# Lp pooling on one Trainium2 core: whole-load squares and sums against chunks, with group 0 stored in two parts

## The chip, the core and the metric

The kernel runs on one NeuronCore of a Trainium2 chip. The core has several engines that run side by side, each with its own instruction queue: ScalarE (ACT in the profile), VectorE (DVE), GpSimd (POOL), TensorE (PE, not used here) and SyncE (SP), which here only starts DMA transfers. Data moves between the chip's main memory (HBM) and the core's working memory (SBUF, 128 partitions) on 16 DMA engines, which all queues share. The metric is the time of one execution on the device in microseconds (us); lower is better.

## The reference: what is computed

The input `x` has the shape 32 x 256 x 4096 in float32, `p` is 2 and the window is 4. Every four neighbours along the last axis give one output:

```python
for i in range(out_length):                      # out_length = 4096 // 4
    window = np.abs(x[:, :, 4*i:4*i + 4]) ** p   # p = 2: squares
    result[:, :, i] = (np.mean(window, axis=-1)) ** (1.0 / p)
```

With p = 2 this is the square root of the mean of four squares. 134.22 MB are read and 33.55 MB written. Nothing is used twice, and windows never overlap, so the input may be taken as one flat row of numbers, cut anywhere at a multiple of four.

## The kernel before, in words

**Tiling.** The flat input is spread over 128 partitions, 262144 columns for each. It is taken in 22 loads: 18 of 13184 columns (6592 KB each), then three of 6592 and one of 5056. A load goes into a slot. There are three slots of 13184 columns (`x_tiles`, L62), used in rotation; slot 18 holds two of the small loads and slot 19 the last two. Loads form groups (`groups`, L41): nine groups of two full loads, one of the three loads of 6592, and one of the last load. The outputs of a group lie together in one of two output tiles (`o_tiles`, L63), and are written to HBM by one store for the group. The outputs of groups 9 and 10 lie in slot 2 (`in_x`, L43), which no later load needs.

**Steps of a load.** ACT squares its columns in place (L123). DVE adds each four neighbours into the output tile: in the first 17 loads with one reduce (L93), from load 17 on with two additions of pairs (L99 and L101). ACT then takes the root with a scale of 1/4, in place in the output tile (L86). The list of chunks in `slots` (L39, L40) says how many columns one square and one sum take: all 13184 in loads 0 to 15, two halves in loads 16 and 17, the whole load in loads 18 to 20, two halves of 2528 in load 21.

**Order.** The order of instructions on each engine is that of the program (`manual_schedule`, L64), and the engines wait for each other by semaphores. In the main loop a root is not emitted at once. It is put on the list `pending`, once per group in general, and comes off it after the square and the sum of the next chunk have been emitted (`LAG`, L44 and L125). The names `FINE` and `ENDS` make the last groups root in smaller pieces: after load 19 (with it the outputs of loads 18 and 19), after load 20, and after each half of load 21.

**Transfers.** Loads are started from SP (L77), and a load of a slot waits until DVE has summed what was in it. Stores of groups 0 to 6 are started from ACT, right after the group's root (L88). The stores of groups 7 to 10 (`late`, L42) are started from SP behind all loads (L137). SP works in order: a store that waits for its root holds up what stands behind it in that queue. The first reduce into an output tile waits until the store of the group that had it before has landed.

Of the kernel before, what the change touches and what calls it, by code (L numbers as in the profile page):

```python
# [1 line left out]

# [4 lines left out]


@with_exitstack
def kernel(  # L10
    ctx: ExitStack,
    tc: tile.TileContext,
    x: bass.AP,
    p: float,
    kernel_size: int,
    out: bass.AP,
):

    nc = tc.nc

    assert float(p) == 2.0, "kernel specialized for p == 2"
    k = int(kernel_size)
    assert k == 4, "kernel specialized for kernel_size == 4"

    P = nc.NUM_PARTITIONS  # L30
    fp32 = mybir.dt.float32
    Act = mybir.ActivationFunctionType
    xf = x.rearrange("b c l -> (b c l)")
    of = out.rearrange("b c l -> (b c l)")
    total = xf.shape[0] // P

    W, O_W = 13184, 6592
    X_SLOTS, O_SLOTS = 3, 2
    slots = [[(W, [W])]] * 16 + [[(W, [6592, 6592])]] * 2  # L39
    slots += [[(6592, [6592]), (6592, [6592])], [(6592, [6592]), (5056, [2528, 2528])]]  # L40
    groups = [2] * 9 + [3, 1]  # L41
    late = {7, 8, 9, 10}  # L42
    in_x = {9: (2, 0), 10: (2, 4944)}  # L43
    FINE, ENDS, LAG = {21}, {19, 20}, 1  # L44
    PAIRS = 17


    loads = [(s, sum(w for w, _ in slot[:j]), *slot[j]) for s, slot in enumerate(slots)
             for j in range(len(slot))]
    n = len(loads)  # L50
    assert sum(w for _, _, w, _ in loads) == total

    firsts = [sum(groups[:g]) for g in range(len(groups))]
    assert sum(groups) == n
    group_of = [g for g, count in enumerate(groups) for _ in range(count)]
    columns = [sum(w for _, _, w, _ in loads[firsts[g]:firsts[g] + groups[g]])
               for g in range(len(groups))]

    x_pool = ctx.enter_context(tc.tile_pool(name="x_pool", bufs=1))
    o_pool = ctx.enter_context(tc.tile_pool(name="o_pool", bufs=1))  # L60

    x_tiles = [x_pool.tile([P, W], fp32, name=f"xt{j}") for j in range(X_SLOTS)]  # L62
    o_tiles = [o_pool.tile([P, O_W], fp32, name=f"ot{j}") for j in range(O_SLOTS)]  # L63
    ctx.enter_context(tc.manual_schedule())  # L64

    def block(flat, g, div):
        at, width = sum(columns[:g]) * P // div, columns[g] * P // div
        return flat[at:at + width].rearrange("(p w) -> p w", p=P)

    xs = {}  # L70

    def load(i):
        s, at, w, _ = loads[i]
        v = x_tiles[s % X_SLOTS][:, at:at + w]
        g = group_of[i]
        src = sum(loads[j][2] for j in range(firsts[g], i))
        nc.sync.dma_start(out=v, in_=block(xf, g, 1)[:, src:src + w])  # L77
        xs[i] = v

    ots = {}  # L80

    def store(g, queue):
        queue.dma_start(out=block(of, g, k), in_=ots[g])  # L83

    def root(g, o, ends):
        nc.scalar.activation(out=o, in_=o, func=Act.Sqrt, scale=1.0 / k)  # L86
        if ends and g not in late:
            store(g, nc.scalar)  # L88

    def total_sum(o, v, i):  # L90
        add = mybir.AluOpType.add
        if i < PAIRS:
            nc.vector.tensor_reduce(  # L93
                out=o, in_=v.rearrange("p (n j) -> p n j", j=k),
                axis=mybir.AxisListType.X, op=add,
            )
            return
        h = v.rearrange("p (m t) -> p m t", t=2)
        nc.vector.tensor_tensor(out=h[:, :, 0], in0=h[:, :, 0], in1=h[:, :, 1], op=add)  # L99
        q = v.rearrange("p (n j) -> p n j", j=k)  # L100
        nc.vector.tensor_tensor(out=o, in0=q[:, :, 0], in1=q[:, :, 2], op=add)  # L101

    ahead = 0
    while ahead < n and loads[ahead][0] < X_SLOTS - 1:
        load(ahead)
        ahead += 1
    pending = []
    done = 0
    for i in range(n):
        s, _, w, chunks = loads[i]  # L110
        while ahead < n and loads[ahead][0] < s + X_SLOTS:
            load(ahead)
            ahead += 1
        g = group_of[i]
        if i == firsts[g]:
            t, first = (o_tiles[g % O_SLOTS], 0) if g not in in_x else (x_tiles[in_x[g][0]], in_x[g][1])
            ots[g] = t[:, first:first + columns[g] // k]
            summed = rooted = 0
        assert sum(chunks) == w
        c = 0  # L120
        for step in chunks:
            v = xs[i][:, c:c + step]
            nc.scalar.activation(out=v, in_=v, func=Act.Square)  # L123
            total_sum(ots[g][:, summed:summed + step // k], v, i)
            while pending and pending[0][0] <= done - LAG:  # L125
                root(*pending.pop(0)[1:])
            done += 1
            c += step
            summed += step // k
            ends = summed == columns[g] // k  # L130
            if ends or i in FINE or (i in ENDS and c == w):
                pending.append((done - 1, g, ots[g][:, rooted:summed], ends))
                rooted = summed
    for job in pending:
        root(*job[1:])
    for g in sorted(late):
        store(g, nc.sync)  # L137


# [1 line left out]
_INS = ['x', 'p', 'kernel_size']  # L141
_OUTS = [((32, 256, 1024), 'float32')]

_NUMBERS = {'p': 2.0, 'kernel_size': 4}


# [26 lines left out]
```

## Time and profile before

The median of 3 runs is 397.92 us (397.87 to 398.24).

| | |
|---|---|
| profiled execution, its own time | 398.24 us |
| its span, from the first instruction to the last | 396.2 us |
| ACT busy | 281.7 us in 40 instructions |
| DVE busy | 275.0 us in 32 instructions |
| DMA, mean rate over the span | 423 GB/s |
| one square of 13184 columns (L123) | 11.19 us |
| one reduce of 13184 columns (L93) | 13.89 us |
| one root of 6592 columns (L86) | 5.68 us |
| a full load, from issue to landing (median) | 31.7 us |
| a store from ACT, from issue to landing (median) | 27.0 us |

"Busy" is the time in which an engine executed an instruction; starting a DMA and waiting are not counted. The span is shorter than the execution's time by what lies ahead of the first instruction and behind the last one. The columns of the windows view are: the stretch and its length, busy time of DVE, ACT and POOL in it with the number of instructions, the clock granted to TensorE, the mean share of time in which the 16 DMA engines were at work, and the rate in GB/s. A packet is counted with its whole size where it starts, so single microseconds may show shares over 1. In the table of waits a row gives the engine and line that waited, what ended the wait, the time in total, how often, and the longest. SPq and ACTq are the queues from which DMAs are started. In lines of the timeline, the first number is the start, the second the duration; square brackets give the idle time before it and what ended that.

### The profile page before, as it was taken

What the parts mean: (1) busy time and instruction counts of PE and PEld (TensorE: products, weight loads), DVE (VectorE), ACT (ScalarE), POOL (GpSimd) and SP (SyncE); (2) the same over time, 40 slices, a digit from 0 to 9 for tenths busy, and PEclk for the clock granted to TensorE, in tenths of its full rate; (3) what the DMA queues carried; (4) which work ended last, traced back from release to release, by engine and by line L of the source; (5) the groups of instructions that cost most, each with busy time, mean ns of one, the idle gap of its engine ahead of it and who ended that gap; (6) DMA issues with size and microseconds to landing.
All of it is one profiled execution on the core that took longest, in us unless ns stands there. A gap on an engine that the chain in (4) does not pass through costs nothing.

```text
span 396.2 us, 192 instructions
## 1 busy us (share of the span) xinstructions
DVE 275.0 (69%) x32; ACT 281.7 (71%) x40; POOL 0.2 (0%) x4
## 2 busy tenths in 40 slices
DVE  0008898685959286929691969396919697699594
ACT  1095689929880998199709972996299639997973
POOL 0000000000000000000000000000000000000000
DMA  8999999999999999999999999999999999999967
GB/s 341 431 442 453 442 437 426 381 431 466 423 407 442 437 426 453 426 437 418 466 426 426 426 415 445 434 453 399 458 453 410 453 426 426 410 445 416 447 269 321
DMA packets 4752, 167.77 MB, mean 423 GB/s; under 512 B 528, under 2 KB 528, under 8 KB 656
## 3 DMA queue, kind: packets, MB, share of 16 engines
q1 hardware_dynamic: 3744, 144.15, 84.5%
q10 hardware_dynamic: 1008, 23.63, 13.8%
HBM read 134.22 MB, written 33.55 MB: 423 GB/s over the span
## 4 chain that ended last, share of the span: by engine, by line
DMA 47%; ACT 24%; DVE 22%; issue 6%; SPq 0%; ACTq 0%
DMA xt<-in_x_dram 47%; ACT xt L123 18%; DVE ot L93 14%; ACT ot L86 6%; DVE xt L99 4%; DVE xt L101 2%; DVE ot L101 2%; ACT xt L86 1%; ACT L86 0%; SPq L77 0%; ACTq L83 0%
## 5 line engine op out<-in xcount | busy, mean ns | idle before, releaser
L93 DVE TENSOR_REDUCE ot<-xt 128x3296 f32<-128x13184 f32 (+1 forms) x18 | 236.2, 13123 | 110.6 <-ACT xt L123 108.9
L123 ACT ACTIVATE xt<-xt 128x13184 f32<-128x13184 f32 (+2 forms) x25 | 223.1, 8937 | 102.0 <-DMA xt<-in_x_dram 100.2
L86 ACT ACTIVATE ot<-ot 128x6592 f32<-128x6592 f32 x9 | 51.2, 5683 | 2.9 <-DVE ot L101 2.9
L99 DVE TENSOR_TENSOR xt<-xt 128x3296 f32<-128x3296 f32 (+1 forms) x7 | 20.9, 2986 | 5.7 <-ACT xt L123 5.7
L101 DVE TENSOR_TENSOR xt<-xt 128x1648 f32<-128x1648 f32 (+1 forms) x5 | 12.1, 2411 | 0.2
L86 ACT ACTIVATE xt<-xt 128x632 f32<-128x632 f32 (+2 forms) x4 | 6.0, 1492 | 5.0 <-DVE xt L101 5.0
L101 DVE TENSOR_TENSOR ot<-xt 128x1648 f32<-128x1648 f32 x2 | 6.2, 3119 | 0.1
L123 ACT ACT_TABLE_LOAD x1 | 1.3, 1283 | 0.7 <-PEq L154 0.7
L86 ACT ACT_TABLE_LOAD x1 | 1.3, 1283 | 0.0
L154 POOL MEMSET const-uint8-127<- 128x1 uint8 x1 | 0.1, 102 | 0.0
L154 POOL MEMSET const-bfloat16-1.0<- 128x1 bf16 x1 | 0.1, 101 | 0.0
L154 POOL MEMSET const-float32-0.0<- 128x1 f32 x1 | 0.1, 98 | 0.2 <-issue 0.2
L154 POOL MEMSET const-float32-1.0<- 128x1 f32 x1 | 0.1, 98 | 0.0
## 6 DMA issues: line engine op xcount, KB each, us to landing
xt<-in_x_dram SPq DMA_DIRECT2D x18, 6592.0 KB, 31.7
out_dram<-ot ACTq DMA_DIRECT2D x7, 3296.0 KB, 27.0
xt<-in_x_dram SPq DMA_DIRECT2D x3, 3296.0 KB, 27.8
out_dram<-ot SPq DMA_DIRECT2D x2, 3296.0 KB, 25.0
xt<-in_x_dram SPq DMA_DIRECT2D x1, 2528.0 KB, 23.0
out_dram<-xt SPq DMA_DIRECT2D x1, 2472.0 KB, 7.3
out_dram<-xt SPq DMA_DIRECT2D x1, 632.0 KB, 3.1
```

What stands on the lines that cost most here:

```text
L86: nc.scalar.activation(out=o, in_=o, func=Act.Sqrt, scale=1.0 / k)
L93: nc.vector.tensor_reduce(out=o, in_=v.rearrange("p (n j) -> p n j", j=k), axis=mybir.AxisListType.X, op=add,)
L99: nc.vector.tensor_tensor(out=h[:, :, 0], in0=h[:, :, 0], in1=h[:, :, 1], op=add)
L101: nc.vector.tensor_tensor(out=o, in0=q[:, :, 0], in1=q[:, :, 2], op=add)
L123: nc.scalar.activation(out=v, in_=v, func=Act.Square)
L154: nc = _bacc.Bacc("TRN2", target_bir_lowering=False, num_devices=1)
```

## The change

Every load is now cut into chunks: the 18 full ones into 4416, 4384 and 4384 columns, the loads of 6592 into two of 3296, and the last one, as before, into two of 2528. Every chunk has one square, one reduce and one root; the root of a chunk stands on ACT behind the square of the next chunk. The additions of pairs, `FINE`, `ENDS`, `LAG` and `PAIRS` are gone. The first chunk of group 0 is stored by itself as soon as it is rooted (1104 outputs, 4.4 KB per partition), and the rest of that group in a second store (5488 outputs); the other groups still have one store each. The tiles of slots and outputs are no longer made once: each load slot and each group asks a rotating pool for one, and the outputs of groups 9 and 10 take the next two places in the rotation of the slots. In the changed program the loads of slot 19 wait for the last reduce of slot 16; before, each waited for one of its two reduces.

```diff
--- before.py
+++ after.py
@@ -36,13 +37,11 @@
 
     W, O_W = 13184, 6592
     X_SLOTS, O_SLOTS = 3, 2
-    slots = [[(W, [W])]] * 16 + [[(W, [6592, 6592])]] * 2
-    slots += [[(6592, [6592]), (6592, [6592])], [(6592, [6592]), (5056, [2528, 2528])]]
+    slots = [[(W, [4416, 4384, 4384])]] * 18
+    slots += [[(6592, [3296, 3296])] * 2, [(6592, [3296, 3296]), (5056, [2528, 2528])]]
     groups = [2] * 9 + [3, 1]
     late = {7, 8, 9, 10}
-    in_x = {9: (2, 0), 10: (2, 4944)}
-    FINE, ENDS, LAG = {21}, {19, 20}, 1
-    PAIRS = 17
+    in_x = {9, 10}
 
 
     loads = [(s, sum(w for w, _ in slot[:j]), *slot[j]) for s, slot in enumerate(slots)
@@ -56,22 +55,22 @@
     columns = [sum(w for _, _, w, _ in loads[firsts[g]:firsts[g] + groups[g]])
                for g in range(len(groups))]
 
-    x_pool = ctx.enter_context(tc.tile_pool(name="x_pool", bufs=1))
-    o_pool = ctx.enter_context(tc.tile_pool(name="o_pool", bufs=1))
-
-    x_tiles = [x_pool.tile([P, W], fp32, name=f"xt{j}") for j in range(X_SLOTS)]
-    o_tiles = [o_pool.tile([P, O_W], fp32, name=f"ot{j}") for j in range(O_SLOTS)]
+    x_pool = ctx.enter_context(tc.tile_pool(name="x_pool", bufs=X_SLOTS))
+    o_pool = ctx.enter_context(tc.tile_pool(name="o_pool", bufs=O_SLOTS))
     ctx.enter_context(tc.manual_schedule())
 
     def block(flat, g, div):
         at, width = sum(columns[:g]) * P // div, columns[g] * P // div
         return flat[at:at + width].rearrange("(p w) -> p w", p=P)
 
+    slot_tiles = {}
     xs = {}
 
     def load(i):
         s, at, w, _ = loads[i]
-        v = x_tiles[s % X_SLOTS][:, at:at + w]
+        if at == 0:
+            slot_tiles[s] = x_pool.tile([P, W], fp32, name="xt")
+        v = slot_tiles[s][:, at:at + w]
         g = group_of[i]
         src = sum(loads[j][2] for j in range(firsts[g], i))
         nc.sync.dma_start(out=v, in_=block(xf, g, 1)[:, src:src + w])
@@ -79,33 +78,26 @@
 
     ots = {}
 
-    def store(g, queue):
-        queue.dma_start(out=block(of, g, k), in_=ots[g])
+    stored = {}
+
+    def store(g, queue, until=None):
+        first = stored.get(g, 0)
+        until = columns[g] // k if until is None else until
+        queue.dma_start(out=block(of, g, k)[:, first:until], in_=ots[g][:, first:until])
+        stored[g] = until
 
     def root(g, o, ends):
         nc.scalar.activation(out=o, in_=o, func=Act.Sqrt, scale=1.0 / k)
         if ends and g not in late:
             store(g, nc.scalar)
-
-    def total_sum(o, v, i):
-        add = mybir.AluOpType.add
-        if i < PAIRS:
-            nc.vector.tensor_reduce(
-                out=o, in_=v.rearrange("p (n j) -> p n j", j=k),
-                axis=mybir.AxisListType.X, op=add,
-            )
-            return
-        h = v.rearrange("p (m t) -> p m t", t=2)
-        nc.vector.tensor_tensor(out=h[:, :, 0], in0=h[:, :, 0], in1=h[:, :, 1], op=add)
-        q = v.rearrange("p (n j) -> p n j", j=k)
-        nc.vector.tensor_tensor(out=o, in0=q[:, :, 0], in1=q[:, :, 2], op=add)
+        elif g == 0 and g not in stored:
+            store(g, nc.scalar, o.shape[1])
 
     ahead = 0
     while ahead < n and loads[ahead][0] < X_SLOTS - 1:
         load(ahead)
         ahead += 1
-    pending = []
-    done = 0
+    pending = None
     for i in range(n):
         s, _, w, chunks = loads[i]
         while ahead < n and loads[ahead][0] < s + X_SLOTS:
@@ -113,26 +105,25 @@
             ahead += 1
         g = group_of[i]
         if i == firsts[g]:
-            t, first = (o_tiles[g % O_SLOTS], 0) if g not in in_x else (x_tiles[in_x[g][0]], in_x[g][1])
-            ots[g] = t[:, first:first + columns[g] // k]
-            summed = rooted = 0
+            pool, width = (o_pool, O_W) if g not in in_x else (x_pool, W)
+            t = pool.tile([P, width], fp32, name="ot" if g not in in_x else "xt")
+            ots[g] = t[:, 0:columns[g] // k]
+        at = sum(loads[j][2] for j in range(firsts[g], i)) // k
         assert sum(chunks) == w
         c = 0
         for step in chunks:
             v = xs[i][:, c:c + step]
             nc.scalar.activation(out=v, in_=v, func=Act.Square)
-            total_sum(ots[g][:, summed:summed + step // k], v, i)
-            while pending and pending[0][0] <= done - LAG:
-                root(*pending.pop(0)[1:])
-            done += 1
+            o = ots[g][:, at + c // k:at + (c + step) // k]
+            nc.vector.tensor_reduce(
+                out=o, in_=v.rearrange("p (n j) -> p n j", j=k),
+                axis=mybir.AxisListType.X, op=mybir.AluOpType.add,
+            )
+            if pending is not None:
+                root(*pending)
             c += step
-            summed += step // k
-            ends = summed == columns[g] // k
-            if ends or i in FINE or (i in ENDS and c == w):
-                pending.append((done - 1, g, ots[g][:, rooted:summed], ends))
-                rooted = summed
-    for job in pending:
-        root(*job[1:])
+            pending = (g, o, i == firsts[g] + groups[g] - 1 and c == w)
+    root(*pending)
     for g in sorted(late):
         store(g, nc.sync)
 
```

## The prediction

> **What bounds the kernel now.** I read the page's first three parts, then the windows, then the waits of SP's queue, and last ACT's order of time near the end.
>
> ```profile
> span 396.2 us, 192 instructions
> DVE 275.0 (69%) x32; ACT 281.7 (71%) x40; POOL 0.2 (0%) x4
> HBM read 134.22 MB, written 33.55 MB: 423 GB/s over the span
> ```
>
> No compute engine is full, and 423 GB/s is a mean over the whole span. Where is it less? The windows view (us, busy of DVE, ACT and POOL, clock, DMA share, GB/s), first in three stages, then microsecond by microsecond:
>
> ```profile
> 2.00:382.00 380.00, 266.60 (x28) 273.80 (x36) 0.00 (x0) 1.00 1.00 431
> 382.00:388.00 6.00, 5.62 (x3) 4.55 (x3) 0.00 (x0) 1.00 0.25 105
> 388.00:396.00 8.00, 2.75 (x2) 2.08 (x3) 0.00 (x0) 1.00 0.85 358
> 382.00:383.00 1.00, 1.00 (x1) 1.00 (x1) 0.00 (x0) 1.00 0.43 185
> 385.00:386.00 1.00, 1.00 (x1) 1.00 (x1) 0.00 (x0) 1.00 0.00 0
> 386.00:387.00 1.00, 0.97 (x2) 1.00 (x2) 0.00 (x0) 1.00 0.00 0
> ```
>
> For 380 us the DMA engines are full at 431 GB/s. Only then do they run dry, for 6 x 0.75 = 4.5 us between 382 and 388. The reason is in the wait table of SP's queue and in ACT's timeline:
>
> ```profile
> SPq L77 <- DVE ot L93: 337.5, 18, 42.6
> SPq L83 <- ACT xt L86: 25.7, 2, 20.2
> ```
>
> ```profile
> 384.95 1.58 ACT L86 ACTIVATE xt<-xt 128x1648 f32<-128x1648 f32 x1 [1.45 <-DVE xt L101]
> 386.43 2.29 ACT L123 ACTIVATE xt<-xt 128x2528 f32<-128x2528 f32 x1
> 388.63 0.71 ACT L86 ACTIVATE xt<-xt 128x632 f32<-128x632 f32 x1
> 391.57 0.73 ACT L86 ACTIVATE xt<-xt 128x632 f32<-128x632 f32 x1 [2.23 <-DVE xt L101]
> ```
>
> The first row looks like the bottleneck and is not: loads wait long for a slot, but the transfers ahead of them keep the engines full. The second counts: the store of group 9 waits for the root that ends at 386.53, that of group 10 for the one that ends at 392.30. The chain of waits agrees: DMA for long stretches, and from 340 us ACT and DVE in turns. So 380 us are bound by bytes, and the end by ACT and DVE.
>
> **What the Trainium skill says.** "ScalarE: Activation LUTs", section "What ACT_TABLE_LOAD costs": with immediate scale and bias an activation takes 186 ns + 0.833 ns per column. The trace agrees: 11.19 us for 13184 columns is 10.99 + 0.20, 0.72 for 632 is 0.53 + 0.19. "VectorE: DVE Perf Modes", section "The perf-mode tier table": a reduce has only the slowest mode. Here 13.886 us for 13184 columns and 7.020 for 6592 give 1.042 ns per column and 0.153 us per instruction. "DMA: Bandwidth & Descriptors", section "Queues, rings and completion order": each DMA engine takes packets from its queues in turn. Here a 3296 KB store takes 27 us beside loads, while from one landing to the next at the end, on one queue, it is 7.7 us.
>
> **Durations for the new shapes**, from these two lines: square of 4416 columns 3.88 us, 4384 3.85, 3296 2.95, 2528 2.29; root of 1104 or 1096 1.11, 824 0.89, 632 0.72; reduce of 4416 4.75, 4384 4.72, 3296 3.59, 2528 2.79.
>
> **Part by part.**
>
> *Chunks.* 25 squares, 13 roots and 32 DVE instructions become 62 of each. ACT: 86 more at 0.20 = +17.2 us, to about 299. DVE: 273.1 us for 262144 columns + 62 x 0.153 = 282.6, +7.6. Both hide behind 380 us of full DMA. A slot costs ACT 3.88 + 2 x 3.85 + 3 x 1.11 = 14.9 us and DVE 14.2, while its load and its share of a store cost DMA 8.44 MB / 431 = 19.6. Where only loads run it is 15.7, which ACT still just meets. Without that cover these would cost their 17 us.
>
> *Slot release.* From landing to the last reduce a slot was held 11.19 + 13.89 = 25.1 us. Now ACT paces it: 3.88 + 2 x (1.11 + 3.85) + 4.72 = 18.5. Loads are issued some 6 us earlier, behind others that still run. Worth nothing, as the engines are full already.
>
> *Roots and stores on ACT.* A root follows the square of the next chunk, so a group's store leaves about 5 us after the next load lands (the square, the root), where it was 18 (11.2 + 5.7, and waits). It landed just late once, for 1.7 us before the reduce at 328.98; that goes, and was hidden too.
>
> *The split store.* Root of chunk one at about 29.3, then one more DMA issue, 0.38 us on ACT. Queued behind it are slot 0's third square, its reduce and the fourth load, which is still issued at about 38.5 instead of 44.63. The bytes are the same. What a further store start costs among loads isn't shown alone. After the first store (issued 68.86) the rate is 316 GB/s in 72 to 76 us and 468 in 76 to 84: 1.1 us lost against 431, then 0.7 regained. So 0 to 1.1 us; I take 0.4. A gain is excluded, as bytes don't fall.
>
> *Tiles from rotating pools.* The two last outputs get the buffers of slots 17 and 18, whose readers are earlier on the same DVE. The load of slot 19 now waits for all of slot 16, not for its halves: both loads at about 342 instead of 336.02 and 346.85. They are wanted when the load before them ends, at 356.0. Cost 0, with 14 us in hand. Some loads also wait for a store four groups back, which has landed some 65 us earlier.
>
> *Pair sums become reduces* from slot 17's second half: 6592 columns took 3.59 + 3.15 = 6.74 us and now 7.18, over four such +1.8 us on DVE. It is hidden behind ACT, as the next sum shows.
>
> **The end, step by step.** All bytes before the last full load are the same and the engines are full, so it lands at 340.36 (issue 310.08 + 30.28) as before, and those after it by queue order: 348.2, 356.0, 363.85, 369.86, store 7 at 377.7, store 8 at 385.45 (issue 365.88 + 19.57). From 340.36 ACT must run, up to the last root of group 9: squares 3.88 + 2 x 3.85 + 6 x 2.95 + 2.29 = 31.6; roots 4 x 1.11 + 6 x 0.89 = 9.8; 20 gaps of 0.02 = 0.4; two waits for DVE, where the next square is shorter than the reduce (0.7 after slot 17, 0.4 at the last chunk) = 1.1. Sum 42.8: group 9's store is issued at 383.2, not 386.55. After it come a square (2.29), a root, a reduce (2.79) and a root: group 10's at about 389.0, not 392.32. Store 8's root is over at 360, needed at 377.7.
>
> A store issued alone (group 10: 3.07 us, of which 632 KB at 431 GB/s is 1.5) has some 0.7 us ahead of its data and 0.8 behind. The slowest DMA engine then ends store 8's data at 385.45 - 0.8 = 384.6, and group 9's packets are queued by 383.9: no gap on that engine. Its end is 385.45 + 2472 KB at 431 GB/s (5.9) + 1.5 = 392.9, against 395.39. Gain 2.5. The DMA sets the end again.
>
> Sum: -2.5 + 0.4 = -2.1, span 394.1. The profiled execution took 398.24 around a span of 396.2, so it becomes 396.1; the median of the runs is 397.92, 0.3 below it, so **395.8 us**, 0.5% faster.
>
> **Rivals.**
>
> *A, the end is ACT's (slower).* The place is ACT between 340 and 389 us, some 24 instructions that alternate with DVE. The price is a delay d at each, beyond the 0.02 us allowed. From 383.9 on, group 9's store comes late and each us counts; at 4 us late, d = 0.17, nothing is gained; at d = 0.25 group 10 is issued at 395, the span ends near 399 and the median is 400.5. For it: ACT meets the loads by under 1 us a slot, so nothing is made up. Against it: in this trace ACT to DVE takes 0.02 to 0.03 us (30.69 to 30.72).
>
> *B, no change.* The many small packets of the split store, and stores that leave earlier, cost the DMA 2 us in turns between queues, all over the run: 397.8. For it: the bound is DMA. Against: seven stores beside loads are in the 431 GB/s already.
>
> *C, more gain.* The split is free and the slowest engine's lag of 2.3 us (its landing after the first one's, 383.14) shrinks: span 393, 394.7.
>
> *D, the early release is worth something in the middle:* no, the share there is 1.00.
>
> **How the numbers follow.** This kernel's measurement tells about 0.2%, 0.8 us, from no change. My forecast (395.0 to 396.6) 0.66; C 0.08; part of the gain (396.6 to 397.1) 0.05; B and what else lands within 397.1 to 398.7 0.10; A 0.11. Faster 0.79, same 0.10, slower 0.11. The range from 394.6 to 398.3 leaves out most of A and tails of C and B, under 0.2.
>
> **What would show it.** Right: the DMA share about 1.00 up to 390 us, no empty microsecond at 385, and group 9's store issued near 383; slots released 18 to 19 us after landing; the last full load landing within 1 us of 340.4. Wrong: that landing later by more than 1 us (then the middle lost DMA time, B), or group 9's store issued after 385 with ACT idle before roots (A). The weakest numbers are the 0.4 us for the split and ACT's two waits.

## The result and the profile after

The changed kernel takes 394.92 us (394.78 to 395.09), the kernel before 398.08 us beside it. The ratio is 0.992, with a 95% interval of 0.991 to 0.993: 0.8% faster. The forecast was 395.8 us, with a range from 394.6 to 398.3. The profiled execution took 395.09 us around a span of 393.3 us. Where the spans are on record, an execution of the kernel before took 2.0 to 2.1 us more than its span, one of the changed kernel 1.7 to 1.8: some 0.3 us of the 3.2 us gained lie outside the span, and nothing here shows why.

First the page's heading lines of the changed kernel, which answer to those shown of before:

```profile
span 393.3 us, 318 instructions
DVE 282.4 (72%) x62; ACT 292.7 (74%) x126; POOL 0.2 (0%) x4
HBM read 134.22 MB, written 33.55 MB: 427 GB/s over the span
```

DVE works 7.4 us longer and ACT 11.0 us longer, and yet the kernel is faster: the total work of neither engine sets the time. The bytes are the same; their mean rate rose from 423 to 427 GB/s. Where, the windows view of the changed kernel says, in the same stages (us, busy of DVE, ACT, POOL, clock, DMA share, GB/s):

```profile
2.00:382.00 380.00, 278.21 (x61) 288.23 (x124) 0.00 (x0) 1.00 1.00 431
382.00:388.00 6.00, 4.16 (x2) 3.16 (x3) 0.00 (x0) 1.00 0.99 425
388.00:396.00 8.00, 0.00 (x0) 0.00 (x0) 0.00 (x0) 1.00 0.33 138
...
385.00:386.00 1.00, 1.00 (x1) 0.00 (x0) 0.00 (x0) 1.00 1.15 494
386.00:387.00 1.00, 0.63 (x1) 0.34 (x1) 0.00 (x0) 1.00 1.01 435
```

The first 380 us are as they were, share 1.00 and 431 GB/s. Between 382 and 388 us the share went from 0.25 to 0.99, and the empty microseconds 385 and 386 are full. What was left over for the last stage is now little. The roots that the last stores wait for, in the timeline of the changed kernel:

```profile
380.72 0.89 ACT L90 ACTIVATE xt<-xt 128x824 f32<-128x824 f32 x1 [0.67 <-DVE xt L118]
381.51 2.30 ACT L116 ACTIVATE xt<-xt 128x2528 f32<-128x2528 f32 x1
381.63 6.12 SPq L86 DMA_DIRECT2D out_dram<-xt  x2
383.71 0.71 ACT L90 ACTIVATE xt<-xt 128x632 f32<-128x632 f32 x1
...
386.66 0.73 ACT L90 ACTIVATE xt<-xt 128x632 f32<-128x632 f32 x1 [2.23 <-DVE xt L118]
```

The SPq line merges two issues: group 9's store at 381.63 us and, when the root of 386.66 ends, group 10's at 387.42. In the kernel before, these were at 386.55 and 392.32:

```profile
386.55 6.11 SPq L83 DMA_DIRECT2D out_dram<-xt  x2
```

The DMA view shows what that does (KB each, us from issue to landing), of the kernel before and then of the changed one:

```profile
out_dram<-xt SPq DMA_DIRECT2D x1, 2472.0 KB, 7.3
out_dram<-xt SPq DMA_DIRECT2D x1, 632.0 KB, 3.1
```

```profile
out_dram<-xt SPq DMA_DIRECT2D x1, 2472.0 KB, 9.3
out_dram<-xt SPq DMA_DIRECT2D x1, 632.0 KB, 5.0
```

Both stores now take 2.0 us longer from issue to landing. They wait behind store 8, so the DMA engines and no longer the roots set the end.

### The profile page after: what moved, and what is told of

It is laid out like the page before. It is cut to its first block, busy times and chain, and to the rows that moved or that the text cites. A ratio compares the mean times of both kernels' runs of the same rounds, so it can differ in the third digit from the quotient of the medians.

```text
span 393.3 us, 318 instructions
## 1 busy us (share of the span) xinstructions
DVE 282.4 (72%) x62; ACT 292.7 (74%) x126; POOL 0.2 (0%) x4
## 4 chain that ended last, share of the span: by engine, by line
DMA 58%; ACT 21%; DVE 16%; issue 2%; another core or an unknown queue 1%; ACTq 0%; SPq 0%
DMA xt<-in_x_dram 58%; ACT xt L116 17%; DVE ot L118 12%; DVE xt L118 3%; ACT ot L90 3%; ACT xt L90 1%; ACTq L86 0%; SPq L76 0%; ACTq L116 0%
## 5 line engine op out<-in xcount | busy, mean ns | idle before, releaser
L118 DVE TENSOR_REDUCE ot<-xt 128x1096 f32<-128x4384 f32 (+1 forms) x54 | 255.4, 4731 | 102.9 <-ACT xt L116 102.6
L116 ACT ACTIVATE xt<-xt 128x4384 f32<-128x4384 f32 (+3 forms) x62 | 230.5, 3718 | 89.2 <-DMA xt<-in_x_dram 85.9
L90 ACT ACTIVATE ot<-ot 128x1096 f32<-128x1096 f32 (+1 forms) x54 | 59.9, 1109 | 1.8 <-DVE ot L118 0.9
L118 DVE TENSOR_REDUCE xt<-xt 128x824 f32<-128x3296 f32 (+1 forms) x8 | 27.0, 3385 | 1.3 <-ACT xt L116 1.2
L90 ACT ACTIVATE xt<-xt 128x824 f32<-128x824 f32 (+1 forms) x8 | 6.8, 844 | 3.0 <-DVE xt L118 2.9
```

Of the source, the lines that this page charges most:

```text
L118: nc.vector.tensor_reduce(out=o, in_=v.rearrange("p (n j) -> p n j", j=k), axis=mybir.AxisListType.X, op=mybir.AluOpType.add,)
```

## The experiments

Two theories are tested. By the first, the one of the prediction, the gain is the gap of the DMA engines in the end, closed because groups 9 and 10 are rooted earlier. By the second, rival 1 (close to the prediction's D), earlier slot release and earlier stores in the middle of the run bring it. Each kernel was timed beside the kernel before, whose median in these comparisons was 398.33 to 398.49 us; ratios are against it.

### The end alone

```diff
-    slots = [[(W, [W])]] * 16 + [[(W, [6592, 6592])]] * 2
-    slots += [[(6592, [6592]), (6592, [6592])], [(6592, [6592]), (5056, [2528, 2528])]]
+    slots = [[(W, [W])]] * 16 + [[(W, [4416, 4384, 4384])]] * 2
+    slots += [[(6592, [3296, 3296])] * 2, [(6592, [3296, 3296]), (5056, [2528, 2528])]]
...
-    FINE, ENDS, LAG = {21}, {19, 20}, 1
-    PAIRS = 17
+    FINE, ENDS, LAG = set(range(16, 22)), set(), 1
+    PAIRS = 22
```

> The kernel before, with the chunks, reduces and single roots of the changed kernel from load 16 on only; loads 0 to 15 stay whole, nothing is split in group 0, the tiles are fixed. Theory (the gain is the gap of the DMA engines in the end, closed because groups 9 and 10 are rooted earlier): most of the gain stays. Load 16 still meets the whole reduce of load 15 and the 5.7 us root of group 7, so the end starts some 2.9 us later than in the changed kernel; the store of group 9 goes out near 384.5 us, that of group 10 near 390.3, and the median is 395.8 to 396.4. Rival 1 (earlier slot release and earlier stores in the middle bring the gain): 397.5 to 398.1, with the last full load at 340.4 us as before.

Measured: 396.05 us, ratio 0.994 (0.993 to 0.996). The last two stores went out at 384.64 and 390.42 us, within 0.2 us of what was expected. The windows view of this kernel:

```profile
2.00:340.00 338.00, 229.68 (x18) 235.65 (x30) 0.00 (x0) 1.00 1.00 430
340.00:382.00 42.00, 40.60 (x11) 40.90 (x21) 0.00 (x0) 1.00 1.01 433
382.00:388.00 6.00, 5.54 (x3) 4.76 (x4) 0.00 (x0) 1.00 0.71 303
```

The middle is untouched, and the share in the gap rises from 0.25 to 0.71. Three quarters of the gain come with the end alone.

### The middle alone

```diff
-    slots = [[(W, [W])]] * 16 + [[(W, [6592, 6592])]] * 2
+    slots = [[(W, [4416, 4384, 4384])]] * 16 + [[(W, [6592, 6592])]] * 2
...
-    FINE, ENDS, LAG = {21}, {19, 20}, 1
+    FINE, ENDS, LAG = set(range(16)) | {21}, {19, 20}, 1
```

> The kernel before, with three chunks and three roots for each of loads 0 to 15 only; from load 16 on it is as before, and group 0 is not split. Theory (end gap): the end keeps its 5.7 us squares and roots, so little is gained: the last full load lands 0 to 0.5 us earlier, the store of group 9 goes out 0.5 to 1 us earlier, and the median is 397.0 to 397.8. Rival 1 (the middle brings the gain): 395.0 to 395.5.

Measured: 396.70 us, ratio 0.996 (0.995 to 0.997): a larger gain than my theory allowed, and not the one of rival 1. In the timeline the cause lies in the end again. These are lines of the kernel before and then of this one, around loads 16 and 17:

```profile
328.50 5.68 ACT L86 ACTIVATE ot<-ot 128x6592 f32<-128x6592 f32 x1
...
334.09 5.68 ACT L123 ACTIVATE xt<-xt 128x6592 f32<-128x6592 f32 x1
339.80 7.02 DVE L93 TENSOR_REDUCE ot<-xt 128x1648 f32<-128x6592 f32 x1 [3.81 <-ACT xt L123]
...
346.74 3.58 DVE L99 TENSOR_TENSOR xt<-xt 128x3296 f32<-128x3296 f32 x1
```

```profile
329.74 1.10 ACT L86 ACTIVATE ot<-ot 128x1096 f32<-128x1096 f32 x1
...
330.74 5.68 ACT L123 ACTIVATE xt<-xt 128x6592 f32<-128x6592 f32 x1
339.78 16.87 ACT L123 ACTIVATE xt<-xt 128x6592 f32<-128x6592 f32 x3 [3.36 <-DMA xt<-in_x_dram]
...
345.51 3.59 DVE L99 TENSOR_TENSOR xt<-xt 128x3296 f32<-128x3296 f32 x1 [1.70 <-ACT xt L123]
```

Before, the 5.68 us root of group 7 stood between the two halves of load 16, and DVE was busy with load 16 until 346.8 us. Rooted in chunks, only 1.10 us are left there, and load 17's sum starts 1.23 us earlier. About half of that is the last full load, which lands at 339.70 us instead of 340.36. Group 9's store goes out at 385.34 us, 1.21 us earlier, and the span is 1.2 us shorter; another 0.3 us of the gain lie outside the span, as in the changed kernel. So the middle does give something, not by DMA share there (1.00, 430 GB/s up to 340 us) but by what it leaves to the end. The gains of the end alone (2.4 us) and of the middle alone (1.7 us) add up to more than the 3.2 us of the whole change: both move the same store.

### The split of group 0's store, taken away and done seven times

```diff
-        elif g == 0 and g not in stored:
-            store(g, nc.scalar, o.shape[1])
```

> The changed kernel, with one store for group 0. Prediction's term for the further store start, 0.4 us: 394.5. If the start costs nothing: 394.8 to 395.0. Rival 2 (the early first store is what moved the last full load from 340.36 to 339.89 us): that landing goes back to 340.3 and the median to 395.3 to 395.5.

```diff
-        elif g == 0 and g not in stored:
+        elif g not in late and g not in stored:
```

> The changed kernel, with groups 0 to 6 all stored in two parts, the first chunk of the group alone and then the rest: six more store starts beside loads, no more bytes. At 0.4 us for a start, as predicted: 394.9 + 2.4 = 397.3, with the last full load landing near 342.3. At 0: 394.9. At the upper end of 1.1 us: 401.5. Rival 2 (an early first part helps): below 394.7.

Measured on the same chip: 394.69 us without a split (ratio 0.991, 0.990 to 0.993), 395.07 us with seven (0.992, 0.991 to 0.993). The medians are 0.38 us apart, which is 0.05 us for each of seven store starts. The intervals overlap, and even their outer ends (0.990 and 0.993, some 1.4 us) leave no more than 0.2 us for a start; the 0.4 us of the prediction was too much. Rival 2 falls too: without the split, the last full load lands at 340.08 us, with seven splits at 339.80, and the time is not the 395.3 us or more that it asked for. The split, which is a visible part of the change, brings none of the gain.

### Which part of the end

```diff
-    slots = [[(W, [W])]] * 16 + [[(W, [6592, 6592])]] * 2
+    slots = [[(W, [W])]] * 16 + [[(W, [4416, 4384, 4384])]] * 2
...
-    FINE, ENDS, LAG = {21}, {19, 20}, 1
+    FINE, ENDS, LAG = {16, 17, 21}, {19, 20}, 1
```

> The kernel before, with loads 16 and 17 alone in three chunks with a root each; loads 18 to 20 stay whole with pair sums and roots as before. Theory (the end is a chain of ACT and DVE whose steps are the chunks and roots): the 5.7 us root of group 8 becomes three of 1.1 us and no longer stands between the squares of loads 18 and 19, but squares of 5.7 us stay; group 9's store goes out near 385.4 us instead of 386.55, group 10's near 391.3, and the median is 396.8 to 397.3 where the kernel before has 398.1. If the root of group 8 alone were the cause, all of the gain: 395.5 or less.

Measured: 396.02 us, ratio 0.995 (0.994 to 0.996), 0.8 us better than the range expected; the stores went out at 384.35 and 390.13 us, some 1 us earlier than I had summed. Part of that is the last full load, which landed at 339.91 us here, 0.45 us earlier than in the kernel before. Up to load 15 the two programs are the same, so this part is scatter from one execution to the next: in the end-alone kernel, again the same up to there, it landed at 340.84.

The median is that of the end-alone kernel (396.05 us), though loads 18 to 20 stay whole here. The medians of the spans are 394.2 us here and 393.8 there, so the fine chunks of loads 18 to 20 (there with reduces in place of pairs) are worth some 0.4 us; nearly all that the end alone gives comes with loads 16 and 17 and the root of group 8 in pieces.

```diff
-    slots += [[(6592, [6592]), (6592, [6592])], [(6592, [6592]), (5056, [2528, 2528])]]
+    slots += [[(6592, [3296, 3296])] * 2, [(6592, [3296, 3296]), (5056, [2528, 2528])]]
...
-    FINE, ENDS, LAG = {21}, {19, 20}, 1
+    FINE, ENDS, LAG = {18, 19, 20, 21}, set(), 1
```

> The kernel before, with loads 18 to 20 alone in two chunks each and a root for each chunk; loads 16 and 17 in halves with one 5.7 us root for group 8, as before. Theory: that root now stands behind the square of only half of load 18, so DVE, which waits 4.6 us for ACT behind it in the kernel before, waits longer: group 9's store goes out near 388.3 us, group 10's near 393.5, and the median is 398.5 to 399.8, slower than the kernel before. Rival (fine chunks at the very end are what gains): 395.5 to 396.5.

Measured: 399.60 us, ratio 1.003 (1.002 to 1.005), slower than before, as expected. Its timeline:

```profile
360.41 5.70 ACT L86 ACTIVATE ot<-ot 128x6592 f32<-128x6592 f32 x1 [5.71 <-DVE ot L101]
...
366.01 2.93 ACT L123 ACTIVATE xt<-xt 128x3296 f32<-128x3296 f32 x1
...
368.98 1.88 DVE L99 TENSOR_TENSOR xt<-xt 128x1648 f32<-128x1648 f32 x1 [5.12 <-ACT xt L123]
...
388.24 6.11 SPq L83 DMA_DIRECT2D out_dram<-xt  x2
```

ACT first waits 5.71 us for DVE, as group 8's root needs all its sums. Then the root takes 5.70 us, while DVE, which has only half of load 18 squared, waits 5.12 us for ACT. Around one long root both engines stand idle in turn, each for over 5 us. So the fine chunks at the very end lose while this root is whole; with loads 16 and 17 chunked too, as in the end-alone kernel, the end gains.

### Pair sums put back

```diff
-            nc.vector.tensor_reduce(
...
+            if i < 17:
+                nc.vector.tensor_reduce(
...
+            else:
+                h = v.rearrange("p (m t) -> p m t", t=2)
+                nc.vector.tensor_tensor(out=h[:, :, 0], in0=h[:, :, 0], in1=h[:, :, 1], op=mybir.AluOpType.add)
+                q = v.rearrange("p (n j) -> p n j", j=k)
+                nc.vector.tensor_tensor(out=o, in0=q[:, :, 0], in1=q[:, :, 2], op=mybir.AluOpType.add)
```

> The changed kernel, with pair sums from load 17 on as in the kernel before. A pair of 3296 columns takes about 3.5 us where the reduce takes 3.59. Theory (the end is set by the DMA engines, the reduces are hidden behind ACT): 394.7 to 395.0, as the changed kernel. If DVE set the end, some 1 us less: 394.0.

Measured: 394.85 us, ratio 0.992 (0.990 to 0.993): no difference from the changed kernel. Group 9's store went out at 381.05 us, 0.6 us earlier still, and found the DMA engines busy.

### One queue for all stores

```diff
-        while ahead < n and loads[ahead][0] < s + X_SLOTS:
-            load(ahead)
-            ahead += 1
...
-            store(g, nc.scalar)
+            store(g, nc.sync)
...
                 root(*pending)
+            while ahead < n and loads[ahead][0] < s + X_SLOTS:
+                load(ahead)
+                ahead += 1
```

> The changed kernel without the split store, and with the stores of groups 0 to 6 in SP's queue too, each ahead of the load that comes next there: one queue, so that no DMA engine takes turns between two. If the turns cost what the longer packets show (a full-load packet takes 1.958 us in the mean, 1.947 in the median, over 144 on each engine 1.6 us) and let the engines drift apart (1.2 us between the first and the last landing of the first loads, 1.6 to 2.3 at the end), this gives 1 to 2 us: 392.8 to 393.8. If turns cost nothing: 394.7. If SP's waits for roots hold loads up: above 395.

Measured: 396.85 us, ratio 0.997 (0.996 to 0.998). My expectation failed: the kernel takes 1.9 us longer than the changed one, so if the missing turns between two queues gain anything, the new order of transfers loses more. No load came too late (the share is 1.00 up to 382 us), and yet the last full load was late. From the timeline, and from the DMA view of the same load (KB, us to landing), both of this kernel:

```profile
305.29 0.33 SPq L76 DMA_DIRECT2D xt<-in_x_dram  x1
```

```profile
xt<-in_x_dram SPq DMA_DIRECT2D x1, 6592.0 KB, 36.4
```

It landed at 341.7 us; in the changed kernel it was issued at 304.13 us and landed at 339.89. This attempt to beat both kernels made things worse; more on it in the last section.

### The end, put back later

The last test leaves all of the changed kernel as it is, and only delays ACT in the end, with one extra square in the first kernel and three in the second (a range of 3 in place of 1):

```diff
             v = xs[i][:, c:c + step]
+            if i == 21 and c == 0:
+                for _ in range(1):
+                    nc.scalar.activation(out=xs[20][:, :2048], in_=xs[20][:, :2048], func=Act.Square)
```

> The changed kernel, with one more square of 2048 columns (1.9 us on ACT, over data already summed, so it changes no result) ahead of the square of the last load's first half. ACT waited 0.7 us a little later, which takes part of it: group 9's store goes out near 382.9 us instead of 381.6, group 10's near 388.7 instead of 387.4. Theory (in the changed kernel the DMA engines set the end; group 10 lands 5.0 us after its issue where a store issued alone takes 3.06, so 2 us are slack): 394.7 to 395.1, unchanged. Rival (ACT and DVE still set the end): 396.1.

> The same with three such squares, 5.7 us. Group 9's store then goes out near 386.7 us and group 10's near 392.5, as in the kernel before (386.55 and 392.32), with all else as in the changed kernel. Theory (the time of these two stores is the whole difference): the last landing is 392.5 + 3.06 = 395.6, the span 396.4, the median 397.9 to 398.3, the time of the kernel before. Rival 1 (part of the gain is from the middle and stays): 397.4 or less.

Measured: 394.75 us with one square (ratio 0.990, 0.989 to 0.992) and 397.76 us with three (0.998, 0.997 to 0.999). One delay is free. It moved the stores less than expected, to 382.20 and 387.98 us, 0.6 us later than in the changed kernel, as ACT's wait took up part of it and the last full load landed 0.44 us earlier in this profile. They still take 0.9 us longer to land than they do alone (7.3 and 3.1 us), so a little more delay should have been free too. Group 9's and 10's stores in the timeline and the DMA view, with one square:

```profile
382.20 6.11 SPq L86 DMA_DIRECT2D out_dram<-xt  x2
```

```profile
out_dram<-xt SPq DMA_DIRECT2D x1, 2472.0 KB, 8.2
out_dram<-xt SPq DMA_DIRECT2D x1, 632.0 KB, 4.0
```

In the profile of the kernel with three, the stores go out at 386.13 and some 5.8 us later, 391.9 us, and the gap is back. The timeline and the windows view:

```profile
386.13 6.11 SPq L86 DMA_DIRECT2D out_dram<-xt  x2
```

```profile
2.00:382.00 380.00, 276.89 (x60) 289.13 (x124) 0.00 (x0) 1.00 1.00 431
382.00:388.00 6.00, 2.64 (x1) 6.00 (x4) 0.00 (x0) 1.00 0.40 171
388.00:396.00 8.00, 2.93 (x2) 1.65 (x3) 0.00 (x0) 1.00 0.76 318
```

The span is 395.8 us: 391.9, the 3.1 us of a 632 KB store alone, and 0.8. The kernel before had 392.32 and 396.2. The stores are 0.4 us earlier than there, and the span is 0.4 us shorter. Thus the times at which these two stores go out account for the whole difference between the two spans: put them back, and nothing of the gain in the span is left, whatever the middle does. I had expected 386.7 and 392.5, which is in part why the median lies a little under the expected range; it is still above the 397.4 of rival 1. Beside it the kernel before had 398.49 us, 0.7 more: the profiles show these 0.4 in the span, and the other 0.3 lie outside it (2.0 to 2.1 us before, 1.7 to 1.8 here), where the delay brings nothing back.

## Why the prediction was right

**The bound and the place of the gain** were right: full DMA engines up to 382 us, a gap that only the roots of groups 9 and 10 could close. The end-alone kernel shows that most of the gap closes with the chunks of the end (a DMA share of 0.71 in place of 0.25), the delayed one that it opens again without anything else changed.

**The end's sum.** Predicted and measured: last full load 340.36 and 339.89 us, store 8 landed 385.45 and 385.01, group 9's store issued 383.2 and 381.63, group 10's 389.0 and 387.42, last landing 392.9 (393.3 with the split) and 392.45. The step that was mis-sized most is ACT's time from the landing to group 9's last root, 42.8 us against 41.7. Consecutive instructions of ACT overlap: in the timeline of the changed kernel a root starts at 353.45 us, the square ahead of it began at 349.71 and took 3.84, so 0.10 us are shared. The Trainium skill, "ScalarE: Activation LUTs", section "What ACT_TABLE_LOAD costs", states some 93 ns for this; I took the cost per instruction from that place and left the overlap out. In this stretch there are 14 overlaps, 1.3 us in all, where I had added 0.4 us of gaps; ACT's two waits for DVE took 1.6 us and not 1.1. For the same reason ACT rose by 11.0 us and not by 17.2: the durations added up to 16.7 us more, but with 75 overlaps in place of 15. It made no difference to the time, because the end was bound by DMA either way: with one delaying square the same stretch took 42.8 us, and the time did not rise.

**The split store** was costed at 0.4 us and is about 0.05, at most 0.2. That is nearly half of the 0.9 us between forecast and result. The dip after the first store, from which I took it, was not the price of a start.

**Slot release and roots in the middle** were costed at nothing. That holds for the DMA share, but not quite for the end: group 7's long root stood in the way of load 16, and the middle alone gave 1.7 us against the kernel before beside it, 1.2 of them in the profiled spans. In the changed kernel this is part of the same 4.9 us by which group 9's store moved, of which the span shows 2.9.

**Reduces for pairs** and **the later release of slot 16** cost nothing, as predicted: with pairs put back the time is the same, and the loads of slot 19, issued at 342.70 and 343.08 us, landed in queue order. The prediction has the pairs from slot 17's second half on; in the kernel before both halves of load 17 have them, so five such sums changed and not four, by its own figures 2.2 us on DVE and not 1.8, as well hidden. DVE's total, reckoned apart, came out at +7.4 us for +7.6.

**The rivals.** A, an end set by ACT, needed 0.17 us of delay at each instruction; there was none, and the price of its mechanism is what the three squares show. B, costs of turns, did not occur. C, a lag of the slowest DMA engine that shrinks, did in part: the last full load landed 0.47 us earlier, store 8 0.44, and the lag at store 8 fell from 2.3 to 1.6 us. It is the other half of the 0.9 us. (What is left, 0.25 us less outside the span than the 2.0 carried over and a profiled run that lay 0.2 and not 0.3 us above the median, nearly cancels.) The result, 394.92 us, is in the range that was given but just below the forecast's own band of 395.0 to 396.6, and nearest to C's 394.7, which had been given a chance of 0.08: the mechanism was right, the size was missed on two small terms that erred the same way.

## What to carry to other kernels

When the DMA engines are full for nearly the whole run, look for the microseconds in which they are not, and follow the store that ends the gap back to the instruction it waits for. Between two engines that work in turns, one long instruction can leave both idle one after the other (5.7 and 5.1 us here); cut that one first, as finer pieces around it can even lose. Once the transfers queue up at the end, stop: a further 0.6 us on the compute side brought nothing.

## What the runs showed of the hardware that was not expected

The 16 DMA engines do not finish a transfer together, and the last one sets when a load has landed. In the trace each transfer has 16 completion marks, taken here as one for each engine. Of the last full load, the first mark comes at 338.0 to 338.6 us in every kernel, whatever the order of stores; the last one differs. Here the distance from the first mark to the last, one profile each:

| kernel | first load, us | last full load, us |
|---|---|---|
| whole chunks in the middle: before, end alone, slots 16 and 17, slots 18 and 19 | 1.2, 1.2, 1.1, 1.4 | 2.3, 2.4, 1.8, 2.1 |
| three chunks: changed, no split, seven splits, middle alone, pairs, one delay, three delays | 1.2, 1.3, 1.1, 1.1, 1.2, 0.9, 1.2 | 1.6, 1.6, 1.2, 1.3, 1.1, 1.0, 1.3 |
| three chunks, all stores in SP's queue | 1.0 | 3.2 |

With whole chunks the distance grows by 0.6 to 1.2 us over the run, with three chunks by 0.4 at most. It need not grow steadily: in the kernel before it is 3.3 us at the load that lands at 167 us, and from there on it alternates between 3.3 and 2.3 from one load to the next, up to 323 us. In the one-queue kernel it grows with the stores, from 1.0 us to 1.4 after the first and 3.2 at the end, and this is its loss of 1.8 us in the span. Programs that are the same up to load 15 differ by 0.6 us, so a single figure says little; the groups do not overlap. What makes one engine fall behind is not settled: turns between two queues are not needed for it, for it is largest where there is one. That stores which start earlier from ACT's queue go with a smaller distance is seen in these eleven profiles, and no more than that.
